# Modulation vectors as row dot products, the gate row broadcast through DRAM

## The chip, the cores and the metric

One Trainium2 chip, one core. The metric is device time in microseconds (us) of one execution; the kernel before takes 2568.09 us, the median of three runs (2566.07 to 2568.38). Engines: PE (matmul; PEld is its weight load), DVE (vector), ACT (scalar), POOL (unused here) and SP, which in this kernel issues all DMAs from one queue in program order. Each engine runs its own instructions in order and waits for others by semaphores.

## The reference

A transformer of four layers on 256 tokens of width 1024, followed by one more block with a memory. All numbers are fp32. In each layer three sublayers (an FFN, a mixer, an FFN) are modulated by a conditioning vector `c`. Cut to what matters here:

```python
cond = jax.nn.silu(c)
for i in range(DEPTH):
    mod = (cond @ w_mod[i] + b_mod[i]).reshape(-1, N_SUBLAYERS, N_MOD, D_MODEL)
    ...
def _sublayer(x, fn, mod_j, g, b, weight):
    shift, scale, gate = mod_j[:, 0, None, :], mod_j[:, 1, None, :], mod_j[:, 2, None, :]
    y = fn(x * (1 + scale) + shift)
    return _layernorm(DEEPNORM_ALPHA * x + weight * gate * y, g, b)
```

So there are 4 x 3 x 3 = 36 vectors of 1024 numbers, each a product of `cond` (1024) with a matrix of 1024 x 1024 (4 MB, read once). Shift and scale act on the input of a sublayer, the gate on its output.

## The kernel before

Tokens lie in two halves of 128 (t = 0, 1) on the 128 partitions. Weights come from DRAM in pieces of 128 x 2048 fp32 (1 MB) into three buffers (`rawp`, NR = 3). ACT casts each half to a high part `whi` (L219) and DVE computes the low part `wlo` (L222); these go into NW = 21 tiles of 128 x 1024 (`wp`). PE multiplies activations, split the same way, in three matmuls per chunk (L252 to L254, L640 to L642). An FFN has 11 blocks; a block takes three pieces, so 12 tiles, 72 matmuls of 512 columns and 8 transposes (L263) of its hidden part.

The modulation work is a background list: generators in `self.bg`, of which `tick` runs one step. An FFN spreads its steps over its blocks; a mixer has a dot in its order string where a step may run, and what is left is run off (`drain`) before the sublayer's end. A sublayer of kind s = 0 (first FFN of a layer) makes five vectors: scale and shift of the next sublayer (`next_cols`), the gate of its own (`rows_for`), and scale and shift of the one after. The last FFN of a layer makes two and its gate, in layer 1 also the gate of layer 2's mixer; a mixer makes its gate if it isn't there yet. The first two vectors are made in the start, beside the memory's keys and values.

One vector takes four pieces of `w_mod`. The piece has the input index on the partitions, so `mod_acc` scales each by the partition's entry of `cond` and adds it to `acc` (128 x 1024): one multiplication (L369) and seven multiply-adds on DVE (L371). The 128 partial sums of each column then have to be added across partitions. A scale or shift is wanted as columns (entry on the partition): `mod_cols` transposes `acc` in eight pieces of 128 on PE (L263) and sums each on DVE (L383). A gate is wanted as a row on all partitions: `gate_row` loads the bias row broadcast (L332), splits `acc` on ACT and DVE (L419, L420), multiplies both parts by a matrix of ones on PE (L423, L424) and adds the bias on DVE out of PSUM (L425).

At the end of a sublayer `post_ln` reads the gate row (L528) and the normalised result is transposed and scaled by the columns G and B. The order of instructions on each engine is made when the program is built: a scheduler places them by priority and by when operands and buffers come free, so the SP queue's order need not be that of the code.

Of the kernel before, what the change touches and what calls it, by code (L numbers as in the profile page):

```python
# [10 lines left out]
F32 = mybir.dt.float32  # L11
F32R = mybir.dt.float32r
BF16 = mybir.dt.bfloat16
I32 = mybir.dt.int32
AF = mybir.ActivationFunctionType
OP = mybir.AluOpType
AX = mybir.AxisListType

P = 128
D = 1024  # L20
DEPTH = 4
# [8 lines left out]
KIND = [0, 1, 2, 0]  # L30
NEG = -1e30
WLO, ACH, WHI, NRM = 384, 1024, 1024, 512
NR, NW, NT, NH = 3, 21, 12, 10
NAC, NAH = 4, 3
T_FIRST, T_LAST = 4, 20
EARLY = (2,)
# [127 lines left out]
class Net:  # L164
# [189 lines left out]
        while self.bg:  # L354
            self.tick()

    def mod_acc(self, i, s, m):
        nc = self.nc
        acc = self.tmp([P, 1024], name="acc")
        for u in range(4):  # L360
            raw = self.rawp.tile([P, 2048], F32, tag="raw", name=self.nm("rawm"))
            nc.sync.dma_start(raw, self.A["w_mod"][i, s * 3 + m, u])
            for j in range(2):
                k = 2 * u + j
                sc = self.cond[:, k:k + 1]
                for q in range(0, 1024, ACH):
                    src, o = raw[:, j * 1024 + q:j * 1024 + q + ACH], acc[:, q:q + ACH]
                    if k == 0:
                        nc.vector.tensor_scalar(o, src, sc, None, op0=OP.mult)  # L369
                    else:  # L370
                        nc.vector.scalar_tensor_tensor(o, src, sc, o, OP.mult, OP.add)  # L371
            yield
        self.acc = acc

    def mod_cols(self, i, s, m):
        nc = self.nc
        yield from self.mod_acc(i, s, m)
        acc = self.acc
        yield
        pv = self.small(8, "pv")  # L380
        for a in range(0, 8, 4):
            ps = self.transposes(acc[:, a * P:(a + 4) * P], 4)
            nc.vector.tensor_reduce(pv[:, a:a + 4], ps, axis=AX.X, op=OP.add)  # L383
        b = self.bmod[:, (i * 9 + s * 3 + m) * 8:(i * 9 + s * 3 + m + 1) * 8]
        k = i * 3 + s - 1
        if m == 1:
            sc = self.small(8, "sc")
            nc.vector.tensor_tensor(sc, pv, b, OP.add)
            G, B = self.GB[k + 1] = self.small(8, "G"), self.small(8, "B")
            if k < 0:  # L390
                nc.vector.tensor_scalar(G, sc, 1.0, None, op0=OP.add)
            else:
                g, bb = (v[:, k * 8:(k + 1) * 8] for v in (self.lngc, self.lnbc))
                nc.vector.scalar_tensor_tensor(G, sc, 1.0, g, OP.add, OP.mult)
                nc.vector.scalar_tensor_tensor(B, sc, 1.0, bb, OP.add, OP.mult)
        else:
            B = self.GB[k + 1][1]
            if k < 0:
                nc.vector.tensor_tensor(B, pv, b, OP.add)
            else:  # L400
                nc.vector.tensor_tensor(B, B, b, OP.add)
                nc.vector.tensor_tensor(B, B, pv, OP.add)
        yield
# [5 lines left out]

    def gate_row(self, i, s):  # L410
        nc = self.nc
        yield from self.mod_acc(i, s, 2)
        acc = self.acc
        gw = self.tmp([P, D], name="gw")
        self.bcast_row(gw, self.A["b_mod"][i, (s * 3 + 2) * D:(s * 3 + 3) * D], D)
        for q in range(2):
            sl = slice(q * 512, (q + 1) * 512)
            ah, al = self.half([P, 512], F32R, "ah"), self.half([P, 512], F32R, "al")
            nc.scalar.activation(ah, acc[:, sl], AF.Copy)  # L419
            nc.vector.tensor_tensor(al, acc[:, sl], ah.bitcast(F32), OP.subtract)  # L420
            yield
            ps = self.bank("tr", "mod")
            nc.tensor.matmul(ps, self.ones, ah, start=True, stop=False)  # L423
            nc.tensor.matmul(ps, self.ones, al, start=False, stop=True)  # L424
            nc.vector.tensor_tensor(gw[:, sl], ps, gw[:, sl], OP.add)  # L425
        self.gates[i, s] = gw
        yield

# [9 lines left out]
    def setup(self):  # L438
        nc, A, c = self.nc, self.A, self.cst

        def const(name, shape, src=None):
            t = c.tile(shape, F32, name="k_" + name)
            nc.sync.dma_start(t, A[name] if src is None else src)
            return t

        cT = const("cT", [P, 8])
        self.ident = const("ident", [P, P])
        self.mem = []
        for t in range(2):
            m = self.tmp([P, 1024], name="m")  # L450
            nc.sync.dma_start(m, A["mem_2"][t])
            self.mem.append(m)
        self.mg = const("mem_norm_g_2", [P, 8])
        self.bmod = const("b_modT", [P, 288])
        self.cond = c.tile([P, 8], F32, name="cond")
        nc.scalar.activation(self.cond, cT, AF.Silu)
        self.ones = c.tile([P, P], F32R, name="ones")
        onesf = self.half([P, P], name="onesf")
        nc.vector.memset(onesf, 1.0)
        nc.vector.tensor_copy(self.ones, onesf)  # L460

    def setup_x(self):
        c = self.cst
# [935 lines left out]
    def run(self):  # L1399
        nc, A = self.nc, self.A  # L1400
# [19 lines left out]
        k = 0  # L1420
        self.gates = {}
        for i in range(DEPTH):
            for s in range(3):
                k += 1
                xc = self.xn
                ended = self.stop is not None and k >= self.stop
                if s != 1:
                    self.bg.append(self.next_cols(k))
                self.bg.append(self.rows_for(i, s))
                if s == 0:  # L1430
                    self.bg.append(self.next_cols(k + 1))
                if s == 2 and i + 1 in EARLY:
                    self.bg.append(self.gate_row(i + 1, 1))

                def done(t, y, i=i, s=s, k=k, ended=ended):
                    if t == 0:
                        self.settle()
                        self.drain()
                        if not ended:
                            self.xn = self.xt(8, not (s == 0 and KIND[i] == 2))  # L1440
                    return self.post_ln(t, y, k, last=ended)

                if s != 1:
                    f = i * 2 + s // 2
                    self.ffn(xc, A["ffn_w_in"][f], A["ffn_w_out"][f], done, 32 if s == 0 else 26 if i + 1 in EARLY else 19)
                elif KIND[i] == 0:
                    self.mla(xc, i // 3, done)
                elif KIND[i] == 1:
                    self.diff(xc, done)
                else:  # L1450
                    self.mamba(xc, done)
                if ended:
                    self.store()
                    return
# [41 lines left out]
def _cols(a, n):  # L1496
    return np.ascontiguousarray(a.reshape(n, P).T)
# [21 lines left out]
def arrange(v):  # L1519
    v = {k: np.asarray(a) for k, a in v.items()}  # L1520
    A = {}
    A["x"] = v["x"].reshape(2, P, D)
    A["cT"] = _cols(v["c"], 8)
    A["positions"] = np.ascontiguousarray(v["positions"].reshape(2, P).T)
    w = v["w_mod"].reshape(DEPTH, 4, 2, P, 9, D)
    A["w_mod"] = np.ascontiguousarray(w.transpose(0, 4, 1, 3, 2, 5)).reshape(DEPTH, 9, 4, P, 2048)
    A["b_mod"], A["ln_g"], A["ln_b"] = v["b_mod"], v["ln_g"], v["ln_b"]
    A["b_modT"] = _cols(v["b_mod"], 288)
    A["ln_gT"], A["ln_bT"] = _cols(v["ln_g"], 96), _cols(v["ln_b"], 96)
    A["ffn_w_in"] = _ffn_in(v["ffn_w_in"].reshape(2 * DEPTH, D, 2 * FFN))  # L1530
# [6 lines left out]
    q = v["mla_w_q_up"].reshape(2, 384, 8, 192)  # L1537
    q = np.concatenate([q[..., :128].reshape(2, 384, 1024), q[..., 128:].reshape(2, 384, 512)], axis=2)
# [10 lines left out]
    w = v["ssm_w_in"]  # L1549
    A["ssm_w_z"] = _kblk(w[:, :, :2048], 512, 2)  # L1550
    A["ssm_w_x"] = _kblk(w[:, :, 2048:4096], 512, 2)
    b, c = w[:, :, 4096:4608].reshape(1, D, 4, 1, P), w[:, :, 4608:5120].reshape(1, D, 4, 1, P)
# [41 lines left out]
```

## Time and profile before

| | |
|---|---|
| median of 3 runs | 2568.09 us (2566.07 to 2568.38) |
| profiled execution | 2567.9 us span, 34087 instructions |
| PE busy | 2497.5 us (97%) |
| DVE busy | 2129.1 us (83%) |
| ACT busy | 1286.9 us (50%) |
| DMA | 599.15 MB, mean 233 GB/s |
| `w_mod` loads | 144 pieces of 1 MB, 4.8 us each to landing |

Busy is the union of an engine's instructions; matmuls overlap, so the mean length of a matmul is longer than its pitch. The chain of waits is followed back from the last instruction to what released each step. "Landing" is the time from the issue of a DMA to its completion. PEclk is the granted share of PE's clock.

### The profile page before, as it was taken

The numbers are of one execution on the slowest core, as the hardware profiler recorded it, in microseconds if no ns is written. First come the engines' busy times: TensorE is split into PE (matmuls) and PEld (weight loads), VectorE is DVE, ScalarE is ACT, GpSimd is POOL, SyncE is SP. The second block draws the span as 40 slices with busy tenths as digits, with TensorE's granted clock in tenths as the row PEclk, the third lists the DMA queues.
The fourth block names the chain that finished last, engine by engine and source line by source line (L and its number), as shares of the span: only waits on it lengthen the run. The fifth ranks groups of instructions, "written<-read, shape, count | busy, mean of one in ns | idle before, by whom it ended". The sixth has DMA issues, their size and how long they took to land.

```text
span 2567.9 us, 34087 instructions
## 1 busy us (share of the span) xinstructions
PE 2497.5 (97%) x12252; PEld 2065.0 (80%) x12252; DVE 2129.1 (83%) x4847; ACT 1286.9 (50%) x2005; POOL 0.2 (0%) x4
## 2 busy tenths in 40 slices
PE   7999899999999999999999999999989999999998
PEld 6788688888887788888889778887878888788887
DVE  7888988879898988898989987698898856896754
ACT  3544474444446544544566554454446544555542
POOL 0000000000000000000000000000000000000000
PEclk9999999999999999999999999999999999999999
DMA  8888457848876388688742457658845754444552
GB/s 309 308 340 306 159 194 276 309 169 300 321 267 256 123 299 320 221 299 316 270 158 99 164 202 292 252 211 324 310 166 211 275 179 175 164 157 172 200 180 80
DMA packets 92297, 599.15 MB, mean 233 GB/s; under 512 B 12768, under 2 KB 14432, under 8 KB 24672
## 3 DMA queue, kind: packets, MB, share of 16 engines
q1 hardware_dynamic: 92128, 596.98, 63.5%
q8 instruction: 96, 1.57, 0.2%
q14 instruction: 73, 0.60, 0.1%
HBM read 593.79 MB, written 3.15 MB: 232 GB/s over the span
## 4 chain that ended last, share of the span: by engine, by line
PE 86%; DVE 7%; DMA 3%; ACT 2%; issue 1%; SPq 0%; DVEq 0%; ACTq 0%
PE tr L263 4%; PE y0q L640 3%; PE y0q L642 3%; PE y0q L641 3%; PE y1q L640 3%; PE y1q L642 3%; PE y1q L641 3%; DVE wlo L222 2%; PE hid0t L254 1%; PE hid6t L253 1%; PE hid9t L252 1%; PE hid6t L254 1%; PE hid9t L254 1%; PE hid6t L252 1%; PE hid5t L254 1%; PE hid9t L253 1%
## 5 line engine op out<-in xcount | busy, mean ns | idle before, releaser
L222 DVE TENSOR_TENSOR wlo<-raw,whi 128x384 fp32r<-128x384 f32 (+1 forms) x2385 | 1081.7, 505 | 145.8 <-ACT whi L219 76.0
L219 ACT ACTIVATE whi<-raw 128x1024 fp32r<-128x1024 f32 (+1 forms) x801 | 820.2, 1051 | 377.3 <-DMA raw<-in_ffn_w_in_dram 133.5
L371 DVE SCALAR_TENSOR_TENSOR acc<-rawm,cond,acc 128x1024 f32<-128x1024 f32 x252 | 322.9, 1281 | 13.2 <-DMA rawm<-in_w_mod_dram 8.0
L640 PE MATMUL y1q<-whi,ah 128*128 128x512 f32 x396 | 161.7, 408 | 1.7 <-ACT ah L625 1.7
L640 PE MATMUL y0q<-whi,ah 128*128 128x512 f32 x396 | 156.2, 394 | 0.7 <-ACT ah L625 0.2
L642 PE MATMUL y1q<-whi,al 128*128 128x512 f32 x396 | 156.4, 395 | 0.0
L641 PE MATMUL y0q<-wlo,ah 128*128 128x512 f32 x396 | 155.2, 392 | 0.0
L642 PE MATMUL y0q<-whi,al 128*128 128x512 f32 x396 | 155.2, 393 | 0.0
L641 PE MATMUL y1q<-wlo,ah 128*128 128x512 f32 x396 | 155.0, 391 | 0.0
L625 ACT ACTIVATE ah<-tr 128x256 fp32r<-128x256 f32 x198 | 74.7, 382 | 139.6 <-PE tr L263 136.7
L626 DVE TENSOR_TENSOR al<-tr,ah 128x256 fp32r<-128x256 f32 x198 | 82.0, 418 | 34.5 <-ACT ah L625 33.9
L640 PEld LDWEIGHTS y0q<-whi,ah 128*128 128x128 f32 x396 | 74.4, 188 | 17.1 <-ACT ah L625 2.6
L642 PEld LDWEIGHTS y1q<-whi,al 128*128 128x128 f32 x396 | 74.4, 188 | 15.7
L640 PEld LDWEIGHTS y1q<-whi,ah 128*128 128x128 f32 x396 | 74.5, 188 | 14.8 <-ACT ah L625 2.4
L642 PEld LDWEIGHTS y0q<-whi,al 128*128 128x128 f32 x396 | 74.3, 188 | 14.9 <-DVE al L626 0.2
L641 PEld LDWEIGHTS y0q<-wlo,ah 128*128 128x128 f32 x396 | 74.4, 188 | 14.5
L641 PEld LDWEIGHTS y1q<-wlo,ah 128*128 128x128 f32 x396 | 74.7, 189 | 13.2
L285 ACT ACTIVATE ev<-tr,B,G 128x128 f32<-128x128 f32 x192 | 72.9, 466 | 20.4 <-PE tr L263 20.3
L263 PEld LDWEIGHTS tr<-k_ident,ac 128*128 128x128 f32 x396 | 54.0, 140 | 29.6 <-DVE ac L616 3.0
L263 PE MATMUL tr<-k_ident,ac 128*128 128x128 f32 x396 | 74.5, 273 | 2.5 <-DVE ac L616 2.0
L295 DVE TENSOR_TENSOR tmp<-ev,tmp 128x512 fp32r<-128x512 f32 (+1 forms) x76 | 50.5, 664 | 12.7 <-ACT tmp L287 11.8
L252 PE MATMUL hid0t<-whi,tmp 128*128 128x512 f32 x144 | 56.4, 392 | 1.9 <-ACT tmp L287 1.9
(510 smaller groups left out, 6006.0 us busy)
## 6 DMA issues: line engine op xcount, KB each, us to landing
raw<-in_ffn_w_in_dram SPq DMA_DIRECT2D x176, 1024.0 KB, 4.9
rawm<-in_w_mod_dram SPq DMA_DIRECT2D x144, 1024.0 KB, 4.8
raw<-in_ffn_w_out_dram SPq DMA_DIRECT2D x88, 1024.0 KB, 5.0
raw<-in_w_gate_up_dram SPq DMA_DIRECT2D x22, 1024.0 KB, 4.7
raw<-in_w_in_dram SPq DMA_DIRECT2D x14, 1024.0 KB, 4.7
raw<-in_diff_w_in_dram SPq DMA_DIRECT2D x12, 1024.0 KB, 4.7
raw<-in_w_down_dram SPq DMA_DIRECT2D x11, 1024.0 KB, 4.7
raw<-in_w_kv_mem_dram SPq DMA_DIRECT2D x8, 1024.0 KB, 6.4
```

Of the source, the lines that this page charges most:

```text
L219: nc.scalar.activation(hi[:, q:e], s[:, q:e], AF.Copy)
L222: nc.vector.tensor_tensor(lo[:, q:e], s[:, q:e], hi[:, q:e].bitcast(F32), OP.subtract)
L252: nc.tensor.matmul(ps, xh, hi[:, off:off + n], start=first, stop=False)
L254: nc.tensor.matmul(ps, xl, hi[:, off:off + n], start=False, stop=last)
L263: self.nc.tensor.transpose(ps[:, j, :], src[:, j * P:(j + 1) * P], self.ident)
L285: nc.scalar.activation(src[:, j, :], ps[:, j, :], AF.Identity, scale=sc, bias=bcols[:, c + j:c + j + 1])
L371: nc.vector.scalar_tensor_tensor(o, src, sc, o, OP.mult, OP.add)
L625: nc.scalar.activation(ah, tr, AF.Copy)
L626: nc.vector.tensor_tensor(al, tr, ah.bitcast(F32), OP.subtract)
L640: nc.tensor.matmul(y[t][q], ah[:, k, :], hi[:, sl], start=f, stop=False)
L641: nc.tensor.matmul(y[t][q], ah[:, k, :], lo[:, sl], start=False, stop=False)
L642: nc.tensor.matmul(y[t][q], al[:, k, :], hi[:, sl], start=False, stop=l)
```

## The change

`w_mod` is laid out transposed: a piece now has the output index on the partitions and the whole input index in a row (two output groups of 128 in each piece). `cond` becomes a row of 1024 on every partition (`condrow`), loaded broadcast and passed through Silu. A vector is then eight products of a row of 1024 with `condrow`, each of which writes its sum into one column of `pv` (`accum_out`): the vector comes out as 128 x 8 columns. Scale and shift use it as it is. For a gate the bias is added in columns, `pv` is written to DRAM (`grow`, 8 x 128, so 1024 pieces of 4 bytes), and read back broadcast to 128 partitions as `gw`. The transposes and sums of `mod_cols`, the split, matmuls and addition of `gate_row`, the matrix of ones and the loads of `b_mod` rows go. `condrow` takes 4 KB a partition and one weight tile is given up for it (21 to 20). A vector takes fewer steps, and the step counts handed to the FFNs change with that.

```diff
--- before.py
+++ after.py
@@ -30,7 +30,7 @@
 KIND = [0, 1, 2, 0]
 NEG = -1e30
 WLO, ACH, WHI, NRM = 384, 1024, 1024, 512
-NR, NW, NT, NH = 3, 21, 12, 10
+NR, NW, NT, NH = 3, 20, 12, 10
 NAC, NAH = 4, 3
 T_FIRST, T_LAST = 4, 20
 EARLY = (2,)
@@ -354,34 +354,26 @@
         while self.bg:
             self.tick()
 
-    def mod_acc(self, i, s, m):
+    def mod_dot(self, i, s, m, pv):
         nc = self.nc
-        acc = self.tmp([P, 1024], name="acc")
         for u in range(4):
             raw = self.rawp.tile([P, 2048], F32, tag="raw", name=self.nm("rawm"))
             nc.sync.dma_start(raw, self.A["w_mod"][i, s * 3 + m, u])
             for j in range(2):
-                k = 2 * u + j
-                sc = self.cond[:, k:k + 1]
-                for q in range(0, 1024, ACH):
-                    src, o = raw[:, j * 1024 + q:j * 1024 + q + ACH], acc[:, q:q + ACH]
-                    if k == 0:
-                        nc.vector.tensor_scalar(o, src, sc, None, op0=OP.mult)
-                    else:
-                        nc.vector.scalar_tensor_tensor(o, src, sc, o, OP.mult, OP.add)
+                src = raw[:, j * 1024:(j + 1) * 1024]
+                nc.vector.scalar_tensor_tensor(src, src, 1.0, self.condrow, OP.mult, OP.mult,
+                                               accum_out=pv[:, 2 * u + j:2 * u + j + 1])
             yield
-        self.acc = acc
+
+    def bias_cols(self, i, s, m):
+        o = (i * 9 + s * 3 + m) * 8
+        return self.bmod[:, o:o + 8]
 
     def mod_cols(self, i, s, m):
         nc = self.nc
-        yield from self.mod_acc(i, s, m)
-        acc = self.acc
-        yield
         pv = self.small(8, "pv")
-        for a in range(0, 8, 4):
-            ps = self.transposes(acc[:, a * P:(a + 4) * P], 4)
-            nc.vector.tensor_reduce(pv[:, a:a + 4], ps, axis=AX.X, op=OP.add)
-        b = self.bmod[:, (i * 9 + s * 3 + m) * 8:(i * 9 + s * 3 + m + 1) * 8]
+        yield from self.mod_dot(i, s, m, pv)
+        b = self.bias_cols(i, s, m)
         k = i * 3 + s - 1
         if m == 1:
             sc = self.small(8, "sc")
@@ -409,20 +401,13 @@
 
     def gate_row(self, i, s):
         nc = self.nc
-        yield from self.mod_acc(i, s, 2)
-        acc = self.acc
+        pv = self.small(8, "pv")
+        yield from self.mod_dot(i, s, 2, pv)
+        nc.vector.tensor_tensor(pv, pv, self.bias_cols(i, s, 2), OP.add)
+        row = self.dr.tile([8, P], F32, name=self.nm("grow"))
+        nc.sync.dma_start(row.rearrange("a p -> p a"), pv)
         gw = self.tmp([P, D], name="gw")
-        self.bcast_row(gw, self.A["b_mod"][i, (s * 3 + 2) * D:(s * 3 + 3) * D], D)
-        for q in range(2):
-            sl = slice(q * 512, (q + 1) * 512)
-            ah, al = self.half([P, 512], F32R, "ah"), self.half([P, 512], F32R, "al")
-            nc.scalar.activation(ah, acc[:, sl], AF.Copy)
-            nc.vector.tensor_tensor(al, acc[:, sl], ah.bitcast(F32), OP.subtract)
-            yield
-            ps = self.bank("tr", "mod")
-            nc.tensor.matmul(ps, self.ones, ah, start=True, stop=False)
-            nc.tensor.matmul(ps, self.ones, al, start=False, stop=True)
-            nc.vector.tensor_tensor(gw[:, sl], ps, gw[:, sl], OP.add)
+        nc.sync.dma_start(gw, row.rearrange("(o a) p -> o (a p)", o=1).to_broadcast([P, D]))
         self.gates[i, s] = gw
         yield
 
@@ -443,7 +428,6 @@
             nc.sync.dma_start(t, A[name] if src is None else src)
             return t
 
-        cT = const("cT", [P, 8])
         self.ident = const("ident", [P, P])
         self.mem = []
         for t in range(2):
@@ -452,12 +436,9 @@
             self.mem.append(m)
         self.mg = const("mem_norm_g_2", [P, 8])
         self.bmod = const("b_modT", [P, 288])
-        self.cond = c.tile([P, 8], F32, name="cond")
-        nc.scalar.activation(self.cond, cT, AF.Silu)
-        self.ones = c.tile([P, P], F32R, name="ones")
-        onesf = self.half([P, P], name="onesf")
-        nc.vector.memset(onesf, 1.0)
-        nc.vector.tensor_copy(self.ones, onesf)
+        self.condrow = c.tile([P, D], F32, name="condrow")
+        self.bcast_row(self.condrow, A["crow"], D)
+        nc.scalar.activation(self.condrow, self.condrow, AF.Silu)
 
     def setup_x(self):
         c = self.cst
@@ -1442,7 +1423,7 @@
 
                 if s != 1:
                     f = i * 2 + s // 2
-                    self.ffn(xc, A["ffn_w_in"][f], A["ffn_w_out"][f], done, 32 if s == 0 else 26 if i + 1 in EARLY else 19)
+                    self.ffn(xc, A["ffn_w_in"][f], A["ffn_w_out"][f], done, 26 if s == 0 else 21 if i + 1 in EARLY else 16)
                 elif KIND[i] == 0:
                     self.mla(xc, i // 3, done)
                 elif KIND[i] == 1:
@@ -1520,11 +1501,11 @@
     v = {k: np.asarray(a) for k, a in v.items()}
     A = {}
     A["x"] = v["x"].reshape(2, P, D)
-    A["cT"] = _cols(v["c"], 8)
     A["positions"] = np.ascontiguousarray(v["positions"].reshape(2, P).T)
-    w = v["w_mod"].reshape(DEPTH, 4, 2, P, 9, D)
-    A["w_mod"] = np.ascontiguousarray(w.transpose(0, 4, 1, 3, 2, 5)).reshape(DEPTH, 9, 4, P, 2048)
-    A["b_mod"], A["ln_g"], A["ln_b"] = v["b_mod"], v["ln_g"], v["ln_b"]
+    A["crow"] = v["c"].reshape(D)
+    w = v["w_mod"].reshape(DEPTH, D, 9, 4, 2, P)
+    A["w_mod"] = np.ascontiguousarray(w.transpose(0, 2, 3, 5, 4, 1)).reshape(DEPTH, 9, 4, P, 2048)
+    A["ln_g"], A["ln_b"] = v["ln_g"], v["ln_b"]
     A["b_modT"] = _cols(v["b_mod"], 288)
     A["ln_gT"], A["ln_bT"] = _cols(v["ln_g"], 96), _cols(v["ln_b"], 96)
     A["ffn_w_in"] = _ffn_in(v["ffn_w_in"].reshape(2 * DEPTH, D, 2 * FFN))
```

On PE, in the first FFN after block 3's hidden matmuls (`hid3t1`; `y1q` is the FFN's output, `tr` a transposing bank, `ac` the hidden part, `acc` the partial sums of a vector), before:

```order
L252 MATMUL hid3t1_225_1274<-whi_214_1209,tmp_91_608 128x512
L253 MATMUL hid3t1_225_1274<-wlo_215_1210,tmp_91_608 128x512
L254 MATMUL hid3t1_225_1274<-whi_214_1209,tmp_93_610 128x512
L263 MATMUL tr_229_1304<-k_ident_83,acc_193_1107 128x128 x4
L263 MATMUL tr_230_1310<-k_ident_83,acc_193_1107 128x128 x4
L640 MATMUL y1q0_164_962<-whi_180_1013,ah_204_1183 128x512
L641 MATMUL y1q0_164_962<-wlo_181_1014,ah_204_1183 128x512
```

and now:

```order
L252 MATMUL hid3t1_218_1243<-whi_207_1178,tmp_84_577 128x512
L253 MATMUL hid3t1_218_1243<-wlo_208_1179,tmp_84_577 128x512
L254 MATMUL hid3t1_218_1243<-whi_207_1178,tmp_86_579 128x512
L263 MATMUL tr_226_1283<-k_ident_81,ac_216_1225 128x128 x2
L621 MATMUL y1q0_157_931<-whi_173_982,ah_197_1152 128x512
L622 MATMUL y1q0_157_931<-wlo_174_983,ah_197_1152 128x512
```

The eight transposes of `acc` are gone; the two of `ac` stood there or a little later in both.

On SP, around the gate of the first FFN (`rawm` a piece of `w_mod`, `raw` a piece of weights, `gw` the gate row, `lng` and `lnb` the norm's rows), before:

```order
L211 DMA raw_311_1683<-in_ffn_w_in_dram 128x2048
L211 DMA raw_316_1697<-in_ffn_w_out_dram 128x2048
L362 DMA rawm_324_1740<-in_w_mod_dram 128x2048
L332 DMA gw_325_1744<-in_b_mod_dram 128x1024
L211 DMA raw_341_1829<-in_ffn_w_in_dram 128x2048
L211 DMA raw_346_1843<-in_ffn_w_in_dram 128x2048
L211 DMA raw_351_1857<-in_ffn_w_out_dram 128x2048
L332 DMA lng_359_1900<-in_ln_g_dram 128x1024
L332 DMA lnb_360_1901<-in_ln_b_dram 128x1024
```

and now:

```order
L361 DMA rawm_310_1679<-in_w_mod_dram 128x2048
L361 DMA rawm_311_1683<-in_w_mod_dram 128x2048
L211 DMA raw_325_1763<-in_ffn_w_in_dram 128x2048
L211 DMA raw_330_1777<-in_ffn_w_in_dram 128x2048
L408 DMA grow_315_1729<-pv_280_1532 128x8x1
L211 DMA raw_335_1791<-in_ffn_w_out_dram 128x2048
L410 DMA gw_316_1731<-grow_315_1729 128x1024
L332 DMA lng_317_1733<-in_ln_g_dram 128x1024
L332 DMA lnb_318_1734<-in_ln_b_dram 128x1024
L361 DMA rawm_344_1835<-in_w_mod_dram 128x2048
```

The gate's row was one load of the bias, issued behind the last piece of `w_mod`. Now the write `grow` stands two weight loads behind that piece, then one weight load, then the read `gw`, with `lng`, `lnb` and the next pieces behind it. In the other gates one to four weight loads stand between write and read.

## Rows read from the trace of the kernel before

**Rows 1.** The page: busy time by engine, and the chain that ended last.

```profile
PE 2497.5 (97%) x12252; PEld 2065.0 (80%) x12252; DVE 2129.1 (83%) x4847; ACT 1286.9 (50%) x2005; POOL 0.2 (0%) x4
...
PE 86%; DVE 7%; DMA 3%; ACT 2%; issue 1%; SPq 0%; DVEq 0%; ACTq 0%
```

**Rows 2.** Windows: start, two first FFNs; sums of eight FFNs, then between them.

```profile
core 0: us, PE busy (x) PEld busy (x) DVE busy (x) ACT busy (x) POOL busy (x), PEclk, DMA share, GB/s
0.00:80.00 80.00, 60.42 (x344) 52.58 (x345) 59.51 (x118) 38.00 (x59) 0.20 (x4) 0.94 0.82 312
...
570.00:750.00 180.00, 179.91 (x831) 147.75 (x830) 161.64 (x314) 80.19 (x116) 0.00 (x0) 1.00 0.81 302
...
1690.00:1870.00 180.00, 178.53 (x821) 145.76 (x821) 159.59 (x313) 78.84 (x115) 0.00 (x0) 1.00 0.80 295
...
sum 1440.00, PE 1436.72 PEld 1178.59 DVE 1202.67 ACT 661.26 POOL 0.00; mean PE 179.59 PEld 147.32 DVE 150.33 ACT 82.66 POOL 0.00
...
sum 610.00, PE 576.09 PEld 484.51 DVE 543.25 ACT 360.95 POOL 0.00; mean PE 144.02 PEld 121.13 DVE 135.81 ACT 90.24 POOL 0.00
```

**Rows 3.** Chain of waits near 40 us: start, length, what.

```profile
40.21 6.05 DMA raw<-in_w_kv_mem_dram
```

**Rows 4.** Chain at the transposes of a column vector, 138 us.

```profile
138.45 0.23 PE hid3t L254
138.68 0.87 PE tr L263 x8
```

**Rows 5.** Timeline of PE at a gate's matmuls; start, length, what.

```profile
190.78 0.39 PE L423 MATMUL mod<-ah,ones 128*128 128x512 f32 x1
...
191.71 0.39 PE L640 MATMUL y1q<-whi,ah 128*128 128x512 f32 x1
```

**Rows 6.** Groups of the lines that the change removes.

```profile
L371 DVE SCALAR_TENSOR_TENSOR acc<-rawm,cond,acc 128x1024 f32<-128x1024 f32 x252 | 322.9, 1281 | 13.2 <-DMA rawm<-in_w_mod_dram 8.0
...
L369 DVE TENSOR_SCALAR acc<-rawm,cond 128x1024 f32<-128x1024 f32 x36 | 26.9, 746 | 1.2 <-DMA rawm<-in_w_mod_dram 0.9
...
L383 DVE TENSOR_REDUCE pv<-tr 128x4 f32<-128x512 f32 x48 | 31.2, 682 | 8.4 <-PE tr L263 8.4
...
L420 DVE TENSOR_TENSOR al<-acc,ah 128x512 fp32r<-128x512 f32 x24 | 16.2, 687 | 4.4 <-ACT ah L419 4.4
...
L425 DVE TENSOR_TENSOR gw<-mod,gw 128x512 f32<-128x512 f32 x24 | 16.3, 681 | 6.0 <-PE mod L424 6.0
...
L419 ACT ACTIVATE ah<-acc 128x512 fp32r<-128x512 f32 x24 | 14.7, 625 | 27.5 <-DVE acc L371 27.5
```

**Rows 7.** Single lines, durations min/median/max ns: two-tensor forms, ACT's accumulator read.

```profile
L540 DVE TENSOR_TENSOR x<-r,lng x24: 1158/1216/1226, 287.3 to 2187.8; 128x1024 f32<-128x1024 f32 x24
...
L529 DVE SCALAR_TENSOR_TENSOR r<-x,r x48: 670/683/694, 261.3 to 2180.1; 128x512 f32<-128x512 f32 x48
...
L1143 ACT ACTIVATION_READ_ACCUMULATOR msq<-m x2: 186/186/187, 6.7 to 8.1; 128x1 f32 x2
```

**Rows 8.** Waits of SP's queue: total us, times, longest.

```profile
SPq L211 <- DVE acc L371: 249.4, 88, 18.9
```

**Rows 9.** DMA issues: KB each, median us to landing.

```profile
raw<-in_ffn_w_in_dram SPq DMA_DIRECT2D x176, 1024.0 KB, 4.9
...
subg<-in_diff_subln_g_dram SPq DMA_DIRECT2D x1, 0.5 KB, 4.7
```

**Rows 10.** Timeline of ACT in the start.

```profile
0.73 1.28 ACT L456 ACT_TABLE_LOAD   x1 [0.73 <-PEq L1583]
...
11.16 1.06 ACT L219 ACTIVATE whi<-raw 128x1024 fp32r<-128x1024 f32 x1 [2.89 <-DMA raw<-in_w_kv_mem_dram]
```

**Rows 11.** Chain in the FFN from 1690 us.

```profile
1717.13 4.88 DMA rawm<-in_w_mod_dram
...
1725.02 7.26 DMA raw<-in_ffn_w_in_dram
...
1733.02 6.92 DMA rawm<-in_w_mod_dram
```

## The prediction

> **What bounds the kernel now.** I read the page's shares first [rows 1]. PE is busy 97% of the span and holds 86% of the chain that ended last; DVE has 83% and 7% of the chain; DMA 3%. A share is a mean over stages, so the next view is the table of stages [rows 2]: in the eight FFN stages, 1440 of the 2568 us, PE is busy 1436.7 us, at the full granted clock (1.00). DVE is busy 159 to 162 of 180 us in the four FFNs that come first in a layer (two of them are shown; each computes five modulation vectors) and DMA 80 to 85%. Between the FFNs PE is busy 576.1 of 610 us. So in an FFN stage whatever leaves PE should leave the span, as long as weights still arrive; DVE and DMA have 10 and 15 to 20% in hand there, and the last FFN of a layer has more. In the first 80 us PE is busy for 60.4 us only and DMA for 82% [rows 2]; loads such as the 6.05 us one on the chain set the pace [rows 3]. A ninth FFN at the end has no modulation.
>
> A busy PE need not be a PE at its pace, so I checked the pace in the chain and in PE's timeline. Eight transposes of `acc` take 0.87 us of the chain between matmuls that follow each other every 0.23 us, with no gap [rows 4]. The four `mod` matmuls of a gate start at 190.78 and the next ordinary one at 191.71: 0.93 us [rows 5].
>
> **The change, part by part.**
>
> PE, removed. There are 36 vectors: 24 that end as columns (eight transposes each) and 12 gates (four matmuls each). 24 x 0.87 = 20.9 us and 12 x 0.93 = 11.2 us, together 32.0 us. By stage: 22 column vectors and 9 gates lie in FFNs, 22 x 0.87 + 9 x 0.93 = 27.5 us; 3 gates lie in mixers, 2.8 us; 2 column vectors in the start, 1.7 us. The FFN part I credit in full, since PE there is busy 99.8%. Of the mixers' part I credit two thirds, 1.9 us, because PE idles in them. The start's part I credit at nothing: loads set its pace.
>
> DVE, exchanged. A column vector costs 0.746 + 7 x 1.281 + 2 x 0.681 = 11.1 us now, a gate 0.746 + 7 x 1.281 + 2 x 0.687 + 2 x 0.681 = 12.4 us [rows 6]. The new form is eight products of 1024 elements with a sum beside them, and no reduce, no split and no addition out of PSUM. No row shows DVE with a sum beside a product. Its length without the sum is bounded by a two-tensor operation of the same size, 1.216 us, and by the present one, 1.281 us [rows 6, 7]. Reading the sum out costs between nothing and what ACT pays for the same, 0.19 us [rows 7]. So 1.22 to 1.47 us each; I take 1.32, the shorter length and half of the read. That makes 288 x 1.32 = 380 us, and 2 us of small additions, for the 414 us removed: DVE ends 32 us lower (bounds: 61 lower, 12 higher). A five-vector FFN falls from 161.6 to 157.7 us of DVE in a stage of 175.6 us, 90%; at the upper bound it is 164 us, 93%. So I cost the DVE side at nothing: its cover is the slack behind the weight tiles that PE holds ahead. A rule speaks against this. The Trainium skill, "Vector Engine (DVE) Microarchitecture Reference", section "Points that are easy to get wrong", says that a scalar-tensor-tensor instruction with two non-bf16 SBUF sources has half the throughput, because no read port is left for the accumulator. The present product has two fp32 sources from SBUF and goes at 1024 elements in 1.281 us, and 512 more elements cost 1.216 - 0.683 = 0.53 us in rows of two sources [rows 6, 7]; the trace so far shows no halving, but none of these rows uses the accumulator. By the rule the sum would be that of rival B below; without it, the one here.
>
> ACT loses 24 splits of 0.63 us [rows 6]. It also idled 27.5 us in front of them, waiting for DVE's `acc`, with weight casts queued behind [rows 6]. PE was fed all the same, so this I cost at nothing.
>
> SP, changed. Before, a gate's bias row was loaded with nothing to wait for but its buffer. Now SP issues the column write (it waits for DVE's last sum), one to four weight loads, and then the broadcast read, which waits until the write has landed; behind it stand `lng`, `lnb` and the weight loads. The first wait costs nothing where the rows of the order put it: the weight load behind the write needs the buffer that the same DVE instruction frees, and SP waits on DVE for 250 us over `acc` anyway [rows 8]. The second depends on how long 1024 pieces of 4 bytes take. The nearest row is 128 such pieces, which landed in 4.7 us, like a load of 1 MB in the same traffic (4.9 us) [rows 9]. Lower bound 4.7 us, upper bound eight times that, 38 us; I take 5.5 us, by the nearer row. One load is already under way and the next buffer comes free about 3.4 us on (53 loads in 180 us), so SP is some 2 us late, twelve times. PE has tiles in hand: an FFN block uses 12 tiles in 72 x 0.23 + 8 x 0.11 = 17.4 us, 1.45 us each, and with 8 free of the 20 that is about 11 us. I write 0.2 us a gate, 2.4 us. The broadcast itself replaces one of the same size.
>
> Weight tiles, 21 to 20. Tiles are taken in pairs, so the 21st only let one cast run ahead; one tile is 1.45 us of lead. Over the eight FFNs PE idles 3.3 us now, so the bounds are 0 and 8 x 1.45 = 11.6 us; I take 1.0, near what is lost today.
>
> Start. The row of `c`, broadcast, is 512 KB more in front of the first weights: at 312 GB/s, 1.7 us [rows 2]. ACT gains a Silu of 1024 and a table load before its first weight cast at 11.16 us, where it idles for 2.9 us [rows 10]; if the row lands late, a part of 1.28 + 1.06 us comes on top. Two transposes and reduces leave the chain there. I take +1.7 (bounds -1 and +4).
>
> The PE order changes in places beside the removed instructions, as the program is scheduled anew; I give that +-6 us in the range and nothing in the sum.
>
> Sum: -27.5 - 1.9 + 2.4 + 1.0 + 1.7 = -24.3 us. Against the profiled execution, 2567.9 us, that is 2543.6; the median is 0.2 us above it, so 2544 us. By the bounds and the order its own range is 2534 to 2556.
>
> **Rivals.**
>
> A, the feed takes the bound over in the five-vector FFNs. For it: the chain runs through loads and DVE there (1717 to 1740 us: three loads of 4.9 to 7.3 us in a row) [rows 11], and PE loses 1.5 us in that stage. Against it: DVE and DMA have 10% and more in hand on the mean. If the gain of the four such stages is lost (16 column vectors and 4 gates, 17.6 us), the time is 2561 us.
>
> B, slower: the sum halves the product's pace. Then 1024 elements take 1.07 us more, 2.4 us each. The point from which DVE decides is (175.6 - 161.6 + 56.8) / 40 = 1.77 us per product: there it fills the five-vector stage. At 2.4 us it needs 161.6 - 56.8 + 40 x 2.4 = 201 us, 205 with DVE 98% busy: 25 us over today, four times. Adding 7 us for the FFN with four vectors and 7 in the mixers, less some 10 us that the other FFNs still gain, the time is near 2670 us. For it only the rule named above; against it the pace of today's two-source rows.
>
> C, slower: the write lands late. From about 13 to 15 us of landing on PE has used up its tiles, and each further us costs 12 us in all; 20 us would give about 2604 us. For it: 1024 pieces, eight times those of the nearest row. The Trainium skill, "DMA: Bandwidth & Descriptors", section "Rules for kernel authors", says that a non-contiguous last dimension becomes one descriptor per element. Against it: 128 such pieces are as quick as anything else [rows 9], and the rows fall on 16 engines.
>
> D, nothing changes: the transposes lay in time that PE would have idled, 2563 to 2573 us. The chain's rows speak against it.
>
> E, more than forecast: DVE's 32 us also shorten the stage ends, where PE idles 34 us between FFNs: below 2534 us.
>
> **How the numbers follow.** Forecast 0.60, E 0.07, A 0.13, D 0.05, B 0.10, C 0.05. A comparison of this kernel can tell about 0.2%, 5 us. Faster by more than that (under 2563): the forecast, E and most of A, 0.79. Within it: D and a little of A, 0.07. Slower: B, C and a little of D, 0.14. Leaving out B and C and the tails of E and D, 2 in 10, gives 2528 to 2567.
>
> **What would show it.** PE should have 240 transposes and `mod` matmuls less and its busy time fall by about 32 us, with the FFN stages 4.4 us shorter where five vectors are made and 2.7 us with two and a gate. The product should take 1.2 to 1.5 us; from 1.8 us on DVE should be 95% busy in those stages and PE wait for `wlo`: then B. The write should land within 10 us, and SP's wait before the broadcast should show no PE wait some 10 us later: otherwise C. DVE's busy time should be near 2097 us. If PE's busy time falls and its idle time rises as much in the five-vector FFNs, it is A. I am wrong if the FFN stages keep their length.

## The result and the profile after

The changed kernel takes 2649.49 us, median of 4 runs (2646.51 to 2650.98), against 2567.08 us before: 1.0321 times as long, 95% interval 1.0306 to 1.0336. Forecast was 2544 us. The change is slower, at the place that rival C names, the gate's write to DRAM, and by more than C's 2604 us.

The page of the changed kernel, its shares and its chain, then the span and mean granted clock of its core:

```profile
PE 2496.0 (94%) x12012; PEld 2053.9 (78%) x12012; DVE 2070.3 (78%) x5049; ACT 1273.5 (48%) x1984; POOL 0.2 (0%) x4
...
PE 75%; DVE 10%; DMA 9%; ACT 3%; issue 1%; SPq 0%; DVEq 0%; ACTq 0%
```

```profile
core 0: 2644.7 us, clock 0.978
```

Against [rows 1] PE has exactly the 240 instructions less, and DVE is 59 us less busy, yet PE's busy time is lower by 1.5 us only, and the span is longer. Two things show in the rows. PE idles 148.7 us instead of 70.4. And its mean granted clock is 0.978, against 0.992 before; worked out from these means, PE spends about 116 us at the lower level of 1.2 GHz in place of 41, and what is left of the matmuls runs slower for that time.

Where it is: I cut both traces at the first `hid0t` matmul of each FFN and at the first gate product of its end. The sums of eight FFNs and of the stretches between them, from the same view for before, for after, and for the run without any gate write (below, e3):

```profile
sum 1428.70, PE 1425.38 PEld 1168.26 DVE 1191.78 ACT 667.67 POOL 0.00; mean PE 178.17 PEld 146.03 DVE 148.97 ACT 83.46 POOL 0.00
...
sum 865.00, PE 826.30 PEld 692.31 DVE 763.82 ACT 498.62 POOL 0.00; mean PE 103.29 PEld 86.54 DVE 95.48 ACT 62.33 POOL 0.00
```

```profile
sum 1468.10, PE 1429.76 PEld 1166.59 DVE 1142.55 ACT 656.09 POOL 0.00; mean PE 178.72 PEld 145.82 DVE 142.82 ACT 82.01 POOL 0.00
...
sum 894.90, PE 820.71 PEld 683.21 DVE 753.84 ACT 491.88 POOL 0.00; mean PE 102.59 PEld 85.40 DVE 94.23 ACT 61.49 POOL 0.00
```

```profile
sum 1400.80, PE 1399.16 PEld 1146.19 DVE 1140.15 ACT 649.24 POOL 0.00; mean PE 174.89 PEld 143.27 DVE 142.52 ACT 81.15 POOL 0.00
...
sum 866.60, PE 819.69 PEld 684.63 DVE 756.44 ACT 501.62 POOL 0.00; mean PE 102.46 PEld 85.58 DVE 94.56 ACT 62.70 POOL 0.00
```

The profiled execution is 76.8 us longer than before: 39.4 in the FFNs, 29.9 between them (three of these stretches hold a gate and are 8.6 to 10.5 us longer each), 7.0 in the start, 0.5 at the end. In the FFNs PE idled 3.3 us before and 38.3 now. The end of such a window doesn't always fall on the same matmul: in four FFNs those of after hold 16 matmuls more than those of e3, so by estimate some 14 of the 39.4 us are work that in e3 stands between the FFNs.

**The mechanism, read at one gate.** The chain of waits in the first FFN, from the gate's last products on (start, length, what):

```profile
187.67 1.15 DVE rawm L364 x2
...
188.84 0.18 DVE pv L406
...
189.04 10.36 DMA grow<-pv
...
199.41 0.33 SPq L410
...
201.83 9.87 DMA rawm<-in_w_mod_dram
...
211.79 2.39 DVE rawm L364 x4
...
214.20 5.21 DMA raw<-in_ffn_w_in_dram
...
219.44 1.06 ACT whi L219
...
220.55 0.79 PE hid8t L252
```

The column write lands after 10.4 us; behind it SP issues the broadcast, the norm's two rows and three `w_mod` loads, and the next load of FFN weights needs a buffer that the products of these free. PE gets its tile 31 us after the write. But the load of weights that SP had issued 0.4 us behind the write, without waiting for it, is late too. It landed after 15.2 us, where the median of such loads is 5.2 (DMA issues from 189 to 200 us):

```profile
raw<-in_ffn_w_out_dram SPq DMA_DIRECT2D x1, 1024.0 KB, 15.2
```

Windows of the same stretch show why the transfers are late (columns: start and end, length, PE, PEld, DVE, ACT, POOL busy, granted clock, DMA share, GB/s), then the same time in before:

```profile
183.00:190.00 7.00, 7.00 (x32) 5.82 (x31) 6.20 (x14) 2.40 (x3) 0.00 (x0) 1.00 0.95 373
190.00:200.00 10.00, 10.00 (x47) 8.20 (x46) 5.14 (x13) 2.78 (x4) 0.00 (x0) 1.00 0.80 27
...
207.00:217.00 10.00, 7.80 (x36) 6.07 (x34) 7.15 (x15) 0.89 (x3) 0.00 (x0) 0.99 1.01 401
217.00:223.60 6.60, 3.74 (x9) 2.76 (x10) 5.70 (x13) 3.02 (x4) 0.00 (x0) 0.50 0.97 393
```

```profile
190.00:200.00 10.00, 10.00 (x48) 8.19 (x47) 8.28 (x17) 3.04 (x5) 0.00 (x0) 1.00 0.83 300
```

For 10 us behind the write the core receives 27 GB/s in place of 300, while the DMA share reads 0.80: the engines count as busy and move next to nothing. (Both figures count a packet in full in the window where it begins, which is how a share can read 1.01.) In the packet records of the trace single 8 KB packets of such a stretch take up to 11.2 us; their median over the execution is 0.31, and the longest of before is 1.9. 227 packets take over 3 us, in twelve groups, one behind each gate's write; in before none does. The first gate's rate is among the lowest: behind the twelve writes the slowest 10 us bring 20 to 65 GB/s. The write's own packets are not the long ones: behind the first gate they all begin within 2 us of the issue and take 9 ns each, and the long ones are those of the load that begin after them. PE, which had tiles in hand, starves some 25 us later (7.80 us busy of 10), and its clock is then granted at the lower level (0.50) for 7 us.

SP's wait for the write (total us, times, longest), the landings (KB each, median us), and the new product with the read of its sum (busy us, mean ns):

```profile
SPq L410 <- DMA grow<-pv: 96.0, 9, 11.8
```

```profile
gw<-grow SPq DMA_DIRECT2D x12, 512.0 KB, 5.8
grow<-pv SPq DMA_DIRECT2D x12, 4.0 KB, 12.4
```

```profile
L364 DVE SCALAR_TENSOR_TENSOR rawm<-rawm,condrow 128x1024 f32<-128x1024 f32 x288 | 342.2, 1220 | 14.9 <-DMA rawm<-in_w_mod_dram 14.6
...
L364 DVE DVE_READ_ACCUMULATOR rawm<-rawm,condrow 128x1 f32 x288 | 23.8, 83 | 0.0
```

The write of 4 KB lands after 12.4 us in the median, where the row that the forecast went by showed 4.7 [rows 9], and nine of twelve times SP stood still for it.

### The profile page after: what moved, and what is told of

Read it like the earlier page. It is cut to its first block, busy times and chain, and to the rows that moved or that the text cites. A ratio compares the mean times of both kernels' runs of the same rounds, so it can differ in the third digit from the quotient of the medians.

```text
span 2644.7 us, 33918 instructions
## 1 busy us (share of the span) xinstructions
PE 2496.0 (94%) x12012; PEld 2053.9 (78%) x12012; DVE 2070.3 (78%) x5049; ACT 1273.5 (48%) x1984; POOL 0.2 (0%) x4
## 2 busy tenths in 40 slices
DMA packets 104778, 599.71 MB, mean 227 GB/s; under 512 B 25120, under 2 KB 26784, under 8 KB 37152
## 4 chain that ended last, share of the span: by engine, by line
PE 75%; DVE 10%; DMA 9%; ACT 3%; issue 1%; SPq 0%; DVEq 0%; ACTq 0%
DVE wlo L222 4%; PE tr L263 3%; PE y0q L621 3%; PE y0q L623 3%; PE y0q L622 3%; PE y1q L621 2%; PE y1q L622 2%; PE y1q L623 2%; DMA raw<-in_ffn_w_in_dram 2%; DMA raw<-in_ffn_w_out_dram 2%; DMA grow<-pv 2%; PE hid5t L252 1%; PE hid5t L254 1%; PE hid5t L253 1%; PE hid0t L254 1%
## 5 line engine op out<-in xcount | busy, mean ns | idle before, releaser
L364 DVE SCALAR_TENSOR_TENSOR rawm<-rawm,condrow 128x1024 f32<-128x1024 f32 x288 | 342.2, 1220 | 14.9 <-DMA rawm<-in_w_mod_dram 14.6
L252 PE MATMUL hid7t<-whi,tmp 128*128 128x512 f32 x144 | 60.0, 417 | 13.9 <-ACT whi L219 13.9
```

The lines of the kernel that those rows point to most:

```text
L252: nc.tensor.matmul(ps, xh, hi[:, off:off + n], start=first, stop=False)
L364: nc.vector.scalar_tensor_tensor(src, src, 1.0, self.condrow, OP.mult, OP.mult, accum_out=pv[:, 2 * u + j:2 * u + j + 1])
```

## The experiments

Two theories could explain it: the scattered write itself slows all transfers (theory 1), or SP's wait keeps loads unissued (theory 2). A third puts the loss on the rest of the change. Medians below; ratios are to the kernel before in the same session.

**e1, pieces of 32 bytes.** The gate's weight rows and bias are dealt out as p*8+a, so that one partition's eight sums are neighbours in DRAM (left out below: the broadcast reads the row back in that order, and the weights are laid out for it).

```
-        row = self.dr.tile([8, P], F32, name=self.nm("grow"))
-        nc.sync.dma_start(row.rearrange("a p -> p a"), pv)
+        row = self.dr.tile([P, 8], F32, name=self.nm("grow"))
+        nc.sync.dma_start(row, pv)
```

> The rows of the gate's weights are dealt to the partitions as p*8+a, so that a partition's eight sums are neighbours in DRAM: the write is 128 pieces of 32 bytes, not 1024 of 4; SP still waits for it. Theory 1 (the 4-byte pieces hold up every load behind them: 8 KB packets of 3 to 11 us and 27 to 38 GB/s for 10 us after each of the 12 writes): no such packets, landing about 5 us, and the forecast's 2544 plus the 7 us that the start is longer: 2545 to 2560 us. Theory 2 (SP's wait for the landing alone keeps the loads back): with a wait of some 5 us in place of 12, about half the loss stays: 2595 to 2610 us; with an unchanged landing 2649 us. Theory 3 (the rest of the change starves PE: 20 tiles, the load order, the products): 2640 us and more.

**e2, the write without a wait.** The gate row is read from the bias and nothing from `grow`.

```
-        nc.sync.dma_start(gw, row.rearrange("(o a) p -> o (a p)", o=1).to_broadcast([P, D]))
+        self.bcast_row(gw, self.A["b_mod"][i, (s * 3 + 2) * D:(s * 3 + 3) * D], D)
```

> The 1024 pieces of 4 bytes are written as in the change, but the gate row is read from the bias in DRAM, so nothing waits for the write (the gate leaves out its products). Theory 1: the slow packets stay after all 12 writes, and 2620 to 2650 us. Theory 2: with no wait the loss is gone: 2545 to 2560 us. Theory 3: 2640 us and more.

**e3, no write.** As e2, with the two lines of `row` gone.

> No write at all, and the gate row read from the bias (the gate leaves out its products): what the rest of the change is worth. Theories 1 and 2: 2540 to 2555 us, PE busy near 2465 us and its half-clock time back at 40 us. Theory 3: 2640 us and more, as with the write.

**e4, the pieces 64 bytes apart.** As e2, and:

```
+        row = self.dr.tile([8, P, 16], F32, name=self.nm("grow"))
+        nc.sync.dma_start(row.rearrange("a p e -> p a e")[:, :, 0:1], pv.rearrange("p (a e) -> p a e", e=1))
```

> As the run without a wait, but each of the 1024 pieces of 4 bytes goes 64 bytes from the next in DRAM (the gate leaves out its products). If theory 1 holds because neighbouring pieces from several DMA engines fall into one stretch of 64 bytes and go one after another: no slow packets, 2540 to 2560 us. If it is the number of 4-byte writes alone: as the run without a wait and without the spacing, 2620 to 2650 us.

Measured: e1 2572.35 us (1.0016, interval 1.0005 to 1.0026), e2 2622.55 (1.0216, 1.0184 to 1.0247), e3 2557.12 (0.9957, 0.9939 to 0.9974), e4 2558.57 (0.9966, 0.9953 to 0.9978). The landings of e1, e2 and e4, in this order:

```profile
grow<-pv SPq DMA_DIRECT2D x12, 4.0 KB, 3.5
```

```profile
grow<-pv SPq DMA_DIRECT2D x12, 4.0 KB, 12.7
```

```profile
grow<-pv SPq DMA_DIRECT2D x12, 4.0 KB, 4.7
```

Windows behind the first gate's write, which e2 issues at 190.35 us and e4 at 187.01: e2, then e4 twice:

```profile
190.00:200.00 10.00, 9.05 (x41) 7.12 (x39) 2.96 (x8) 2.01 (x2) 0.00 (x0) 1.00 0.78 45
```

```profile
187.00:190.00 3.00, 3.00 (x15) 2.49 (x14) 1.60 (x4) 2.01 (x2) 0.00 (x0) 1.00 0.69 51
...
190.00:200.00 10.00, 8.04 (x38) 6.34 (x37) 4.44 (x12) 4.50 (x7) 0.00 (x0) 1.00 0.80 300
```

SP's wait for the write in e1:

```profile
SPq L410 <- DMA grow<-pv: 19.5, 9, 3.3
```

Theory 3 falls with e3: without the write the same change is 0.4% faster than before. Theory 1 holds for most of the loss: with nothing waiting for the write (e2) 45 GB/s and 55.5 us over before remain, while the same 1024 pieces with gaps between them (e4) end 1.5 us above e3, which is within the noise. The packets say the same: over 3 us take 227 of 8 KB in after, 271 in e2, and none in e1, e3 and e4. A short stall is left even in e4, 51 GB/s for 3 us and a PE wait of 2.0 us at the first gate that e3 doesn't have. Theory 2 has a share: after less e2 is 27 us, the wait; e2 less e4 is 64 us, the pieces. Together that is 91 of the 92 us by which the changed kernel lies above e3. e1 alone doesn't decide between theories 1 and 2. The 2595 us expected of it under theory 2 took a wait of some 5 us a gate; SP waits 19.5 us in all in place of 96, and a fifth of the 92 us on top of e3 would be 2576 us, near the 2572 measured. The decision rests on e2 and e4, in which nothing waits. But a wait for a quick landing is not free either: e1 lies 13.8 us above e4.

**e5, the gate row from GpSimd's queue.** e1 with `nc.gpsimd.dma_start` for the write and the broadcast.

> The 32-byte pieces again, and the write and the broadcast read of the gate row go from GpSimd's queue, which has nothing else to do, so no weight load stands behind the wait for the landing. If the 14 us that the run with 32-byte pieces lies above the spaced pieces without a wait are SP's wait: 2555 to 2562 us, and the wait in the FFNs gone from SP's rows. If the extra broadcast dependence or the write itself costs them: 2572 us as before. If transfers from GpSimd's queue are dearer than SP's: above 2575 us.

2563.18 us (0.9987, 0.9976 to 0.9999): 9 of the 14 us came back; it ends 1 us above the expected range. So most of what e1 pays goes with the wait on SP. Of the rest this run shows only that between the FFNs it keeps 8.4 us over before where e3 has 1.6.

**e6, e5 with an empty step in the start.**

```
             yield from self.mod_cols(0, 0, 1)
+            yield
             yield from self.mod_cols(0, 0, 0)
```

> As the run from GpSimd's queue, and one empty step after the first modulation vector, which gives the start the step back that the change took from each vector: w_kv_mem's third block is again loaded before three of w_mod's blocks, in the order of before. If the start is longer (86 us to the first FFN against 78) through that order: 5 to 6 us below the run without the step, 2549 to 2556 us. If it is longer through the 512 KB of the row of c and its Silu: no difference.

2562.82 us (0.9986, 0.9974 to 0.9998), the first FFN at 85.0 us: no difference. The order of these loads isn't the cause alone.

**e7, the kernel before with 20 weight tiles** (`NW` 21 to 20).

> The kernel before with 20 weight tiles in place of 21, nothing else. The prediction's term for the tile is 1.0 us with bounds of 0 and 11.6: 2567 to 2570 us if it was right, 2575 us and more if the tile is worth its full lead in the FFNs.

2575.91 us (1.0040, 1.0024 to 1.0055): 9 us, near the upper bound of the term and far from the 1.0 taken. In its profile the start is 2.6 us longer than in before.

**e8 and e10, the pieces 32 and 16 bytes apart** (e4 with 8 and with 4 in place of 16), one execution each.

> 1024 pieces of 4 bytes, each 32 bytes from the next, without a wait (the gate leaves out its products). If pieces that are neighbours in 64 bytes are what goes one after another, two of them share such a stretch: slow 8 KB packets come back in part, landing between 4.7 us (64 bytes apart) and 12.7 us (side by side). If 32 bytes is the stretch: landing near 4.7 us, and about 2558 us.

> 1024 pieces of 4 bytes, each 16 bytes from the next, without a wait (the gate leaves out its products). 32 bytes apart they landed in 5.1 us with few slow packets, side by side in 12.7 us with 460 of them. If what goes one after another are pieces within one stretch of 32 bytes: slow packets come back, fewer than side by side, landing between 6 and 12 us, 2565 to 2610 us. If the stretch is 16 bytes or less: landing near 5 us and about 2556 us.

2555.61 us with a median landing of 5.1 us, and 2564.8 us with 5.2: at either distance the write lands about as quickly as at 64 bytes (4.7). In these three runs the eight rows move apart too, from 0.5 KB to 8, 4 and 2 KB, so the next two runs part the two distances.

**e11, neighbours side by side, the eight rows 16 KB apart,** one execution. As e2, and:

```
+        row = self.dr.tile([8, 4096], F32, name=self.nm("grow"))
+        nc.sync.dma_start(row[:, 0:P].rearrange("a p -> p a"), pv)
```

> 1024 pieces of 4 bytes without a wait (the gate leaves out its products), neighbours side by side as in the change, but each of the eight rows of 128 lies 16 KB from the next, so that the write covers 114 KB of DRAM in place of 4. If pieces side by side are what goes one after another: landing near 12 us, several hundred slow 8 KB packets, 2600 to 2640 us. If it is that all of them fall into 4 KB: landing near 5 us and 2550 to 2565 us.

2810.73 us, far outside both expectations. Its landing and its clock:

```profile
grow<-pv SPq DMA_DIRECT2D x12, 4.0 KB, 29.5
```

```profile
core 0: 2809.0 us, clock 0.948
```

**e14, rows 16 KB apart and neighbours 16 bytes apart,** as e2, one execution.

> 1024 pieces of 4 bytes without a wait (the gate leaves out its products), the eight rows 16 KB apart as in the slowest run, but neighbours 16 bytes apart. If pieces side by side are the trigger: landing near 5 us and 2550 to 2565 us. If the distance of the rows is enough by itself: landing near 29 us and about 2810 us.

2581.3 us; the answer lies between the two:

```profile
grow<-pv SPq DMA_DIRECT2D x12, 4.0 KB, 9.4
```

So both count. At rows 16 KB apart, taking neighbours 16 bytes off one another cuts the landing from 29.5 to 9.4 us; at neighbours 16 bytes apart, moving the rows from 2 to 16 KB raises it from 5.2 to 9.4. That 4-byte pieces side by side hold up the loads behind them is shown; what makes them do so isn't. Nor is it shown whether the loads stall because they stand behind the write in SP's queue or would stall in any: no run sent the 4-byte pieces from another queue.

**e9, the 21st tile given back to e5,** its 4 KB a partition from one `ac` buffer, one buffer of small vectors and `krT`'s own buffer.

> The run from GpSimd's queue with 21 weight tiles; their 4 KB a partition come from one buffer less for ac (3, not 4), five in place of six small-vector buffers, and krT taken from the pool of half tiles. Taking the 21st tile from the kernel before cost 9 us by the medians. If it is worth the same here: 2553 to 2558 us, the fastest kernel that computes everything. If PE has no longer any use for it, or the missing ac buffer takes it back: 2560 to 2567 us.

2564.72 us (0.9988, 0.9979 to 0.9997): no gain. Whether the tile is worth nothing here or the `ac` buffer takes it back, this run can't tell.

**e12, e5 without the row of c.**

```
-        self.bcast_row(self.condrow, A["crow"], D)
-        nc.scalar.activation(self.condrow, self.condrow, AF.Silu)
+        nc.gpsimd.memset(self.condrow, 1.0)
```

> The run from GpSimd's queue with the row of ones in place of the row of c and its Silu (the modulation leaves out c): no 512 KB load and no Silu in front of the first weights. If the start, 7 us longer than before, is so through the row: 4 to 5 us below the run with it, 2557 to 2560 us, and the first FFN begins at 81 us, where the kernel before begins it with 20 tiles. If it is the order of the loads and the tiles: no difference, 2563 us and 85 us.

2563.67 us (0.9987, 0.9975 to 0.9999), the first FFN at 84.1 us against 85.6, and the median doesn't change. The 1.5 us are no more than chance gives: among kernels whose start is the same the first FFN begins at 84.4 (e4) to 86.5 us (e2). So the row's load and Silu aren't shown to cost the start anything.

**e13, all three at once.** e6, the row of c issued behind the first weight loads, and the writes of `kvs` from GpSimd's queue.

> The run from GpSimd's queue with the empty step, with the row of c loaded and sent through Silu behind the first weight casts, and with the writes of kvs to DRAM on GpSimd's queue, so that no weight load of the start stands behind a wait for kvs. If the start is longer by these three together: the first FFN begins at 80 to 82 us in place of 85, and 2556 to 2560 us, below every kernel so far that computes everything. If the start is longer by something else, such as the products in DVE: 85 us and 2563 us.

2558.07 us (0.9967, 0.9953 to 0.9980): the fastest kernel here that computes everything, 0.3% under before and 91 us under the change as made. But its first FFN still begins at 84.8 us: by the profiles its gain on e5 sits in the first FFN and the mixer behind it (1.4 and 3.7 us), and part is lost again later; the two profiled executions lie 1.6 us apart, the medians 5.1. So most of the start's 7 us stays open. One difference shows in both SP timelines: the first piece of the last block of `w_kv_mem` is issued 3 us later (SP's timeline: start, length, what), e13 and then before:

```profile
57.45 2.77 SPq L211 DMA_DIRECT2D raw<-in_w_kv_mem_dram  x2
```

```profile
54.20 0.33 SPq L211 DMA_DIRECT2D raw<-in_w_kv_mem_dram  x1
```

In before its casts stand ahead of the sixteen evacuations on ACT, in e13 behind them. No run moved that alone.

## Why the prediction was wrong

**The step that failed** is the write's term on SP: "I write 0.2 us a gate, 2.4 us." The runs show 91 us in its place, 27 for the wait and 64 for the pieces. Two things in that step were wrong. The smaller is the landing: "Lower bound 4.7 us, upper bound eight times that, 38 us; I take 5.5 us, by the nearer row." It was 12.4 us, inside the bounds. The nearest row was no near one: `subg` is a load from DRAM with each piece into another partition [rows 9], and the new transfer writes to DRAM with pieces of different partitions side by side. e4 makes the point: the number of pieces is the same and the landing is 4.7.

**The larger error is the path.** The forecast and rival C both priced the write as a wait: SP is late, PE lives on its tiles, and from 13 to 15 us of landing it runs dry. Landing at 12.4 us should then have cost next to nothing. But the write also slows the load already issued behind it (15.2 us at the first gate), so for 10 us next to no weights come in, whatever SP does; that is 64 of the 91 us. C had the right place, a chance of 0.05, and the wrong mechanism for its size.

The Trainium skill, "DMA: Bandwidth & Descriptors", section "Rules for kernel authors", was weighed there: one descriptor per element. The trace agrees on the count, 25120 packets under 512 bytes against 12768 before, about 12 x 1024 more. But the count isn't the price: e4 has the same 25120 and ends 1.5 us above e3, which has no write.

**Cover of the wait.** 0.2 us a gate was forecast, 2.4 in all. With a landing of 3.5 us (e1) the kernel stands 13.8 us above e4, 1.15 a gate, and 9 of these go when the wait leaves SP (e5). The cover by the tiles in hand did hold in the FFNs: PE idles 1.4 us there in e1 and 1.6 in e3. Between the FFNs it idles 60.3 us in e1 and 46.9 in e3; the forecast had 0.2 us there for each of three gates, and its cover was worked out for FFN blocks alone. The sums of e1:

```profile
sum 1414.50, PE 1413.08 PEld 1158.25 DVE 1144.84 ACT 657.64 POOL 0.00; mean PE 176.63 PEld 144.78 DVE 143.10 ACT 82.21 POOL 0.00
...
sum 873.10, PE 812.79 PEld 677.67 DVE 753.78 ACT 492.03 POOL 0.00; mean PE 101.60 PEld 84.71 DVE 94.22 ACT 61.50 POOL 0.00
```

How the wait reaches PE there was not traced.

**PE's part was right.** By e3 the eight FFNs lose 27.9 us, forecast 27.5, and the whole kernel 32.9 us of PE's busy time, forecast 32.0. A (feed), B (products) and D (no change) fall there.

**The product was right.** 1.220 us and 0.083 for the sum's read make 1.30, forecast 1.32. The rule of the Trainium skill, "Vector Engine (DVE) Microarchitecture Reference", section "Points that are easy to get wrong", by which two fp32 sources from SBUF with an accumulator halve the pace, doesn't hold in this trace: 1024 elements take the 1.22 us of the two-tensor form [rows 7]. DVE's busy time fell by 59 us, forecast 32: 14 of the difference lie in the products (342.2 + 23.8 for 380; they overlap, 288 x 1.220 would be 351), the rest wasn't traced.

**Smaller terms.** e3's median lies 15.9 us above the forecast without its wait, 2541.2. By its profile that is the start, 7.9 us in place of 1.7 (6.2; the term's bounds were -1 and +4); the stretches between FFNs, 1.6 in place of -1.9 (3.5); the FFNs, 1.4 better than the forecast with its term for the tile; 0.5 at the end; and 7.1 us by which the profiled execution of e3 is under its median. The tile was put at 1.0 and cost 9 us in the kernel before; in the changed one it isn't settled.

## What to carry to other kernels

Price a DMA by what it does to the transfers behind it, not by its own landing alone; before a scattered write is trusted, find a row that writes, in the same pattern of addresses. Where the result of an instruction can be laid out so that one partition's values are neighbours in DRAM (here by dealing the weight rows out as p*8+a before the kernel runs), the 4-byte pieces become 32-byte ones and the stall goes: no 8 KB packet of e1 takes over 2.4 us. A DMA that waits belongs on a queue with nothing behind it, which here gave 9 of 14 us back.

## What was not expected of the hardware

- 1024 writes of 4 bytes, with neighbours side by side: landing 12.4 to 12.7 us and, behind the first gate, a tenth of the load traffic for 10 us. With neighbours 16, 32 and 64 bytes and rows 2, 4 and 8 KB apart: 5.2, 5.1 and 4.7 us. With neighbours side by side and rows 16 KB apart: 29.5 us; with 16 bytes and 16 KB: 9.4 us.
- The small packets themselves look quick, 9 ns each; the time shows in the loads that begin behind them, 8 KB packets of up to 11.2 us for a median of 0.31.
- The DMA share says nothing of what is moved: 0.80 at 27 GB/s, 0.83 at 300.
- A stall of the loads is paid for twice: PE's idle time rose by 78 us, and the time at its lower granted clock from about 41 to 116 us.
- A sum beside a product on DVE costs 83 ns, its read alone.
